# Forgetting attention: one 129-column product for upper probabilities in three of four query groups, the partial sums joined later, the division on GpSimd

## The chip, the cores and the metric

The kernel runs on one core of one Trainium2 chip. The metric is device time in microseconds (us) of one execution; the median of three runs before the change is 1155.76 us. Five engines work side by side, each through its own list of instructions in order: PE (TensorE, matrix products into PSUM), DVE (VectorE), ACT (ScalarE), POOL (GpSimd, which here also issues some transfers) and SP (SyncE, which issues most transfers). They wait for one another through semaphores.

## The reference

One decoder layer over 2048 tokens of width 1024. Eight heads of "forgetting" attention and eight heads of sliding-window attention share one input projection; both outputs are gated, projected, normalised and added to the input. The change lies in the forgetting attention:

```python
def one_block(args):
    qb, cb, n = args
    s = jnp.einsum('bhqd,bhkd->bhqk', qb, kh, preferred_element_type=jnp.float32) * scale
    s = s + cb[..., None] - cum[:, :, None, :]
    ...
    s = jnp.where(causal, s, -jnp.inf)
    p = jax.nn.softmax(s, axis=-1)
    return jnp.einsum('bhqk,bhkd->bhqd', p.astype(vh.dtype), vh)
```

All of it is to come out near f32 accuracy, so the kernel splits each f32 operand into an upper and a lower f16 part and adds three products (upper by upper, upper by lower, lower by upper).

## The kernel before

The program has three long stretches: projections with the sliding-window attention, up to about 450 us; the forgetting attention, from 450 to 987 us; the output projection after that. This text is about the second.

**Groups and steps.** A group is one head and one chunk of 512 queries (four query groups of 128, `u` 0 to 3). It is worked in steps of two key blocks of 128 each: 2, 4, 6 and 8 steps for the four chunks, 20 per head, 160 in all (`Step`). In a step, `scores` makes two pairs of products into the PSUM tile `sta` (L1330, L1331), `exp32` takes the exponential on ACT (L1335), on a diagonal step POOL masks it (L1339), `high` rounds it to the upper f16 part on ACT (L1343), `low` makes the lower part on DVE (L1346), and `pv` multiplies both parts with the values.

**The values.** `vt` holds, for each key block and head, 129 columns (`VW`): 64 of the upper part, a column of ones (64), and 64 of the lower part. The column of ones makes the sum of the probabilities in the same product. `pv` takes, for each key block and each `u`, three products into `poa`, a PSUM tile of four times 65 columns: upper probabilities by the upper values and the ones (65 columns, L1356), upper by lower values (64 columns, L1358, added onto the same columns), lower probabilities by upper values and ones (65 columns, L1359). There are 1088 pairs of a key block and a `u`; 768 of them belong to the first three `u`, 320 to the fourth. At the last step of a group DVE takes the reciprocal of the sums (L1363) and multiplies (L1365) into `ona`, and SP stores it (L1366). There is one `poa`: the next group's first product waits until DVE has read it.

**The order** is written out by hand in the loop over `steps`: in iteration s come `exp32` of s, a tick, `low` of s-1, the first half of the filling work, `high` of s, `scores` of s+1, a second tick, `pv` of s-2 (`PV_LAG`), the second half of the filling work. `after(n, f)` puts `f` off to the n-th tick from there. The filling work is products of later heads (L335, with their evacuations) and the search for row maxima of the next head's scores (products L1281, maxima on DVE L1284 and L1286), and it uses the PSUM tiles `bk`.

Of the kernel before, what the change touches and what calls it, by code (L numbers as in the profile page):

```python
# [10 lines left out]
F32 = mybir.dt.float32  # L11
# [3 lines left out]
AF = mybir.ActivationFunctionType  # L15
ALU = mybir.AluOpType
AX = mybir.AxisListType

P = 128
# [4 lines left out]
CH = 512  # L24
# [9 lines left out]
XM, XR, VW = 66, 69, 129  # L34
# [6 lines left out]
def hybrid_layer(  # L41
# [17 lines left out]
    V, A, G, PE, SP = nc.vector, nc.scalar, nc.gpsimd, nc.tensor, nc.sync  # L59
# [15 lines left out]
    o_d = [dram.tile([CH, D], F32, name=f"o_d{t}") for t in range(NCH)]  # L75
# [4 lines left out]
    def sm(n, tag):  # L80
        return small.tile([P, n], F32, tag=tag, name=tag)
# [106 lines left out]
    def after(n, f):  # L188
        late.append([n, f])
# [10 lines left out]
    first = ("kb", "vb", "zb0", "zb1")  # L200
# [253 lines left out]
    start = ExitStack()  # L454
# [241 lines left out]
    def swa_pool(name, bufs, **kw):  # L696
        return swa.enter_context(tc.tile_pool(name=name, bufs=bufs, reuse_waits="tile", **kw))

    op_ = swa_pool("op", 3)
# [149 lines left out]
    class Pair:  # L849
# [73 lines left out]
        def pv(self):  # L923
            j, i = self.j, self.i
            po = ps_pv.tile([P, 4, 64], F32, tag="pv", name="pob")
            for e, (i_, k0, nk) in enumerate(self.blocks):
                for h in range(2):
                    for b in range(nk):
                        for n, (pp_, vv) in enumerate(((0, 0), (0, 1), (1, 0))):
                            PE.matmul(po[:, 2 * e + h, :], self.ptt[:, pp_, self.at[e] + h * nk + b, :],  # L930
                                      vb[:, k0 + b, self.g, 64 * vv:64 * vv + 64],
                                      start=(b == 0 and n == 0), stop=(b == nk - 1 and n == 2))

            def out_():
                on = onp.tile([P, 2, P], F32, tag="on", name="on")
                V.tensor_tensor(on[:].rearrange("p e (h d) -> p (e h) d", h=2), po[:],
                                self.rinv[:].unsqueeze(2).broadcast_to([P, 4, 64]), op=ALU.mult)
                G.dma_start(o_d[i // 4][(i % 4) * P:(i % 4 + 2) * P, (4 + j) * P:(5 + j) * P]
                            .rearrange("(e p) c -> p e c", p=P), on[:])

            after(1, out_)
# [220 lines left out]
    def fox_pool(name, bufs, **kw):  # L1162
        return fox.enter_context(tc.tile_pool(name=name, bufs=bufs, reuse_waits="tile", **kw))

    ps_st = fox_pool("ps_st", 1, space=PSUM)
    ps_po = fox_pool("ps_po", 1, space=PSUM)
# [4 lines left out]
    op_ = foxl.enter_context(tc.tile_pool(name="opa", bufs=2, reuse_waits="tile"))  # L1171
# [77 lines left out]
    vt, lk, lq = fx["vt"], fx["lk"], fx["lq"]  # L1249
# [62 lines left out]
    class Step:  # L1312
# [35 lines left out]
        def pv(self):  # L1348
            hd, ph = self.hd, self.ph
            if self.first:  # L1350
                self.po_[0] = ps_po.tile([P, 4, 65], F32, tag="po", name="poa")
            po = self.po_[0]
            for n, (b, u0, o) in enumerate(self.blocks):
                for u in range(u0, 4):
                    pq = slice(o + (u - u0) * P, o + (u - u0 + 1) * P)
                    PE.matmul(po[:, u, :], ph[:, 0, pq], vt[:, b, hd, 0:65],  # L1356
                              start=(self.first and n == 0 and u == 0), stop=False)
                    PE.matmul(po[:, u, 0:64], ph[:, 0, pq], vt[:, b, hd, 65:VW], start=False, stop=False)  # L1358
                    PE.matmul(po[:, u, :], ph[:, 1, pq], vt[:, b, hd, 0:65], start=False,  # L1359
                              stop=(self.last and n == len(self.blocks) - 1))  # L1360
            if self.last:
                rinv = sm(4, "a_ri")
                V.reciprocal(rinv[:], po[:, :, 64])  # L1363
                on = op_.tile([P, 4, 64], F32, tag="ona", name="ona")
                V.tensor_tensor(on[:], po[:, :, 0:64], rinv[:].unsqueeze(2).broadcast_to([P, 4, 64]), op=ALU.mult)  # L1365
                SP.dma_start(o_d[self.ci][:, hd * 64:(hd + 1) * 64].rearrange("(u p) d -> p u d", p=P), on[:])  # L1366

        po_ = {}

# [213 lines left out]
    with tc.manual_schedule():  # L1583
# [29 lines left out]
        for s, stp_ in enumerate(steps):  # L1613
            hd, r = divmod(s, NS)
# [115 lines left out]
```

## Time and profile before

| | |
|---|---|
| median of three runs | 1155.76 us (1154.94 to 1155.79) |
| the profiled execution, its own time | 1155.56 us |
| its span in the trace | 1153.9 us |
| granted TensorE clock, mean | 0.995 |
| instructions | 27043 |
| ACT busy | 679.0 us (59%) |
| POOL busy | 166.4 us (14%) |

The time of the profiled execution is 1.66 us more than the span, which runs from the first to the last recorded instruction. "Busy" is the time in which an engine has an instruction in work; for PE the ends are modelled and products overlap, so that the start of one to the start of the next tells the pace, not the duration. In rows of a timeline the first column is the start in us from the span's start, the second the duration; a bracket names the idle time before it and what ended it.

### The profile page before, as it was taken

What the parts mean: (1) busy time and instruction counts of PE and PEld (TensorE: products, weight loads), DVE (VectorE), ACT (ScalarE), POOL (GpSimd) and SP (SyncE); (2) the same over time, 40 slices, a digit from 0 to 9 for tenths busy, and PEclk for the clock granted to TensorE, in tenths of its full rate; (3) what the DMA queues carried; (4) which work ended last, traced back from release to release, by engine and by line L of the source; (5) the groups of instructions that cost most, each with busy time, mean ns of one, the idle gap of its engine ahead of it and who ended that gap; (6) DMA issues with size and microseconds to landing.
All of it is one profiled execution on the core that took longest, in us unless ns stands there. A gap on an engine that the chain in (4) does not pass through costs nothing. (4 is left out here: it accounts for less than half of the span.)

```text
span 1153.9 us, 27043 instructions
## 1 busy us (share of the span) xinstructions
PE 1113.2 (96%) x10514; PEld 651.5 (56%) x10514; DVE 909.9 (79%) x2330; ACT 679.0 (59%) x1124; POOL 166.4 (14%) x302
## 2 busy tenths in 40 slices
PE   5899999999999999999999999999999989999997
PEld 1466657655579865555555555555555555455554
DVE  6776668879888477889888989878797886766666
ACT  4666446556666515766767667676776698233331
POOL 2011122234322101111111201101010010000000
PEclk9999999999999999999999999999999999999999
DMA  9646426587777423323233232313121264464642
GB/s 330 223 138 169 107 71 135 111 171 141 174 145 121 96 61 84 85 78 81 78 82 98 61 89 63 66 38 98 43 56 38 66 185 154 156 211 166 203 168 88
DMA packets 162452, 136.36 MB, mean 118 GB/s; under 512 B 95356, under 2 KB 139428, under 8 KB 162324
## 3 DMA queue, kind: packets, MB, share of 16 engines
q1 hardware_dynamic: 152388, 106.39, 35.3%
q0 software_dynamic: 9456, 27.72, 9.1%
q8 instruction: 82, 1.34, 0.5%
q10 hardware_dynamic: 480, 0.53, 0.2%
q14 instruction: 46, 0.38, 0.1%
HBM read 70.97 MB, written 25.18 MB: 83 GB/s over the span
## 5 line engine op out<-in xcount | busy, mean ns | idle before, releaser
L1335 ACT ACTIVATE p<-sta,lift,scl_qk 128x1024 f32<-128x1024 f32 (+2 forms) x160 | 172.0, 1075 | 94.6 <-PE sta L1331 88.7
L335 PE MATMUL bk<-hT,wh_qk 128*128 128x512 f16 x768 | 197.9, 378 | 0.6 <-DVE a_m L1284 0.6
L1503 PE MATMUL bk<-wohl,oz 128*128 128x512 f16 (+2 forms) x792 | 172.5, 372 | 2.2 <-DVE oz L1490 1.0
L1346 DVE TENSOR_TENSOR pha<-p,pha 128x1024 f16<-128x1024 f32 (+2 forms) x160 | 169.7, 1061 | 0.0
L1343 ACT ACTIVATE pha<-p 128x1024 f16<-128x1024 f32 (+2 forms) x160 | 148.1, 926 | 31.6 <-POOL p L1339 26.3
L1284 DVE TENSOR_REDUCE a_m<-bk 128x1 f32<-128x512 f32 x192 | 129.3, 683 | 36.3 <-PE bk L1281 35.4
L1503 PEld LDWEIGHTS <-oz 128*128 128x128 f16 x792 | 75.8, 99 | 83.2 <-issue 1.8
L1356 PE MATMUL poa<-vt,pha 128*128 128x65 f16 x1088 | 116.5, 193 | 1.6 <-DVE ona L1365 1.6
L1359 PE MATMUL poa<-vt,pha 128*128 128x65 f16 x1088 | 116.0, 192 | 1.3 <-DVE pha L1346 1.3
L1358 PE MATMUL poa<-vt,pha 128*128 128x64 f16 x1088 | 116.3, 194 | 0.0
L1330 PE MATMUL sta<-T 128*128 128x512 f16 (+1 forms) x320 | 109.6, 347 | 4.5 <-ACT p L1335 4.5
L1281 PE MATMUL bk<-T 66*128 66x512 f16 (+2 forms) x320 | 110.5, 348 | 2.2 <-DVE a_m L1284 2.2
L1356 PEld LDWEIGHTS <-pha 128*128 128x128 f16 x1088 | 101.6, 97 | 16.3 <-DVE ona L1365 2.9
L335 PEld LDWEIGHTS <-wh_qk 128*128 128x128 f16 x768 | 70.2, 97 | 71.6 <-issue 2.9
L1358 PEld LDWEIGHTS <-pha 128*128 128x128 f16 x1088 | 101.0, 97 | 13.4
L1331 PE MATMUL sta<-T 69*128 69x512 f16 (+1 forms) x320 | 108.0, 348 | 0.0
L1359 PEld LDWEIGHTS <-pha 128*128 128x128 f16 x1088 | 100.8, 99 | 1.6 <-DVE pha L1346 1.6
L335 PE MATMUL bk<-hT,wh_za 128*128 128x512 f16 x384 | 99.8, 378 | 0.0
L353 PE MATMUL bk<-wh_va,hT 128*128 128x128 f16 x1536 | 92.6, 219 | 0.0
L1339 POOL TENSOR_SCALAR_AFFINE_SELECT p<-p 128x256 f32<-128x256 f32 x64 | 31.9, 499 | 413.4 <-ACT p L1335 408.5
L335 PE MATMUL bk<-hT,wh_zb 128*128 128x512 f16 x384 | 90.8, 379 | 0.0
L353 PEld LDWEIGHTS <-hT 128*128 128x128 f16 x1536 | 87.5, 98 | 5.9 <-issue 3.5
(497 smaller groups left out, 1851.5 us busy)
## 6 DMA issues: line engine op xcount, KB each, us to landing
hT<-in_x_dram SPq DMA_DIRECT2D x20, 512.0 KB
wa<-in_w_ada_dram SPq DMA_DIRECT2D x16, 512.0 KB
T<-stq SPq DMA_DIRECT2D x128, 64.0 KB
T<-z_d SPq DMA_DIRECT2D x16, 512.0 KB
T<-o_d SPq DMA_DIRECT2D x16, 512.0 KB
z_d<-tz POOLq DMA_DIRECT2D x30, 256.0 KB, 2.9
out_dram<-hT SPq DMA_DIRECT2D x15, 512.0 KB
xt<-in_x_dram SPq DMA_DIRECT2D x12, 512.0 KB
```

Of the source, the lines that this page charges most:

```text
L335: PE.matmul(ps, whl[:, a, k, :], hT[ci][:, b, k, :], start=(k == 0 and n == 0), stop=(k == KT - 1 and n == 2))
L353: PE.matmul(ps[:, u * P:(u + 1) * P], hT[ci][:, a, k, u * P:(u + 1) * P], whl[:, b, k, :], start=(k == 0 and n == 0), stop=(k == KT - 1 an ...
L1281: PE.matmul(mx[:, :w], T[0:XM, 0, i * P:(i + 1) * P], T[0:XM, 2, pc * CH:pc * CH + w], start=True, stop=True)
L1284: V.tensor_reduce(m3[:, u, pc:pc + 1], mx[:, :w], axis=AX.X, op=ALU.max)
L1330: PE.matmul(self.st[:, o:o + w], T[:, 3, kb_], T[:, 1, qc], start=True, stop=False)
L1335: A.activation(self.p32[:, :self.w], self.st[:, :self.w], AF.Exp, scale=scl[f"qk{self.hd}"][:], bias=lift[:])
L1343: A.activation(self.ph[:, 0, :self.w], self.p32[:, :self.w], AF.Copy)
L1346: V.tensor_tensor(self.ph[:, 1, :self.w], self.p32[:, :self.w], self.ph[:, 0, :self.w], op=ALU.subtract)
L1356: PE.matmul(po[:, u, :], ph[:, 0, pq], vt[:, b, hd, 0:65], start=(self.first and n == 0 and u == 0), stop=False)
L1358: PE.matmul(po[:, u, 0:64], ph[:, 0, pq], vt[:, b, hd, 65:VW], start=False, stop=False)
L1359: PE.matmul(po[:, u, :], ph[:, 1, pq], vt[:, b, hd, 0:65], start=False, stop=(self.last and n == len(self.blocks) - 1))
L1503: PE.matmul(py, self.hl[:, i, k, :], w_slot(8 * j + k)[:, cc], start=(k == 0 and m_ == 0), stop=(k == KT - 1 and m_ == 2))
```

## The change

The tile `poa` becomes 512 columns wide. For `u` 0, 1 and 2 it holds 129 columns each: the upper probabilities are multiplied with all 129 columns of `vt` in one product, and the lower probabilities are added onto the first 65. For `u` = 3 the room is 65 columns (3 x 129 + 65 = 452), and the three products stay as they were. The sum over the upper and the lower values, which the products made before, is now taken after the group for the first three `u`: two copies on ACT (`by_u` columns 65 to 128, and the 64 columns of `u` 3) into `ona`, two reciprocals and one addition on DVE (`join`). The division is a product on POOL, followed by the store (`out_`). `join` stands at the first tick after the group's last `pv`, `out_` at the second.

```diff
@@ -1348,22 +1348,37 @@
         def pv(self):
             hd, ph = self.hd, self.ph
             if self.first:
-                self.po_[0] = ps_po.tile([P, 4, 65], F32, tag="po", name="poa")
+                self.po_[0] = ps_po.tile([P, CH], F32, tag="po", name="poa")
             po = self.po_[0]
             for n, (b, u0, o) in enumerate(self.blocks):
                 for u in range(u0, 4):
                     pq = slice(o + (u - u0) * P, o + (u - u0 + 1) * P)
-                    PE.matmul(po[:, u, :], ph[:, 0, pq], vt[:, b, hd, 0:65],
-                              start=(self.first and n == 0 and u == 0), stop=False)
-                    PE.matmul(po[:, u, 0:64], ph[:, 0, pq], vt[:, b, hd, 65:VW], start=False, stop=False)
-                    PE.matmul(po[:, u, :], ph[:, 1, pq], vt[:, b, hd, 0:65], start=False,
-                              stop=(self.last and n == len(self.blocks) - 1))
+                    c, first = u * VW, self.first and n == 0 and u == 0
+                    stop = self.last and n == len(self.blocks) - 1
+                    if u < 3:
+                        PE.matmul(po[:, c:c + VW], ph[:, 0, pq], vt[:, b, hd, 0:VW], start=first, stop=False)
+                    else:
+                        PE.matmul(po[:, c:c + 65], ph[:, 0, pq], vt[:, b, hd, 0:65], start=False, stop=False)
+                        PE.matmul(po[:, c:c + 64], ph[:, 0, pq], vt[:, b, hd, 65:VW], start=False, stop=False)
+                    PE.matmul(po[:, c:c + 65], ph[:, 1, pq], vt[:, b, hd, 0:65], start=False, stop=stop)
             if self.last:
+                on = op_.tile([P, 4, 64], F32, tag="ona", name="ona")
                 rinv = sm(4, "a_ri")
-                V.reciprocal(rinv[:], po[:, :, 64])
-                on = op_.tile([P, 4, 64], F32, tag="ona", name="ona")
-                V.tensor_tensor(on[:], po[:, :, 0:64], rinv[:].unsqueeze(2).broadcast_to([P, 4, 64]), op=ALU.mult)
-                SP.dma_start(o_d[self.ci][:, hd * 64:(hd + 1) * 64].rearrange("(u p) d -> p u d", p=P), on[:])
+                by_u = po[:, 0:3 * VW].rearrange("p (u c) -> p u c", u=3)
+
+                def join():
+                    A.activation(on[:, 0:3, :], by_u[:, :, 65:VW], AF.Copy)
+                    A.activation(on[:, 3, :], po[:, 3 * VW:3 * VW + 64], AF.Copy)
+                    V.reciprocal(rinv[:, 0:3], by_u[:, :, 64])
+                    V.reciprocal(rinv[:, 3:4], po[:, 3 * VW + 64:3 * VW + 65])
+                    V.tensor_tensor(on[:, 0:3, :], by_u[:, :, 0:64], on[:, 0:3, :], op=ALU.add)
+
+                def out_():
+                    G.tensor_tensor(on[:], on[:], rinv[:].unsqueeze(2).broadcast_to([P, 4, 64]), op=ALU.mult)
+                    SP.dma_start(o_d[self.ci][:, hd * 64:(hd + 1) * 64].rearrange("(u p) d -> p u d", p=P), on[:])
+
+                after(1, join)
+                after(2, out_)
 
         po_ = {}
```

In PE's list the first products of the first head's second group, with what they wait for (`pha` is the pair of probability parts, `poa` the PSUM tile, `sta` the scores; the names behind "waits" are engines' semaphores). Before:

```order
L1331 LDWEIGHTS T_6393
L1331 MATMUL sta<-T_6393 128x128
L1356 LDWEIGHTS pha [waits DVE_49]
L1356 MATMUL poa<-vt,pha 128x65 [waits PE_49]
L1358 LDWEIGHTS pha
L1358 MATMUL poa<-vt,pha 128x64
L1359 LDWEIGHTS pha
```

And now, at the same place:

```order
L1331 LDWEIGHTS T_6393
L1331 MATMUL sta<-T_6393 128x128
L1359 LDWEIGHTS pha [waits DVE_49,PE_49]
L1359 MATMUL poa<-vt,pha 128x129 [waits Activation_49]
L1363 LDWEIGHTS pha
L1363 MATMUL poa<-vt,pha 128x65
```

Three pairs of a weight load and a product became two for `u` 0 to 2; the wait for DVE is at a group's first weight load in both, and the first product now also waits for ACT, which reads `poa` too. (The new L1359 is the wide product, the new L1363 the one of the lower probabilities.)

In DVE's list the end of the first head's fourth group (the `pha` rows are `low` of two steps in sequence, the L1256 to L1261 rows are `key_limbs` of the next head). Before:

```order
L1346 TENSOR_TENSOR pha<-p_7913,pha 128x896
L1363 RECIPROCAL a_ri<-poa 128x4
L1365 TENSOR_TENSOR ona<-poa,a_ri 128x256
L1284 TENSOR_REDUCE a_m<-bk_139 128x1
L1256 TENSOR_SCALAR a_cv<-csum,isc_qk_7604 128x16
L1258 TENSOR_SCALAR lk<-a_cv 128x16
L1261 SCALAR_TENSOR_TENSOR a_cv<-lk,a_cv 128x16
L1258 TENSOR_SCALAR lk<-a_cv 128x16
L1261 SCALAR_TENSOR_TENSOR a_cv<-lk,a_cv 128x16
L1258 TENSOR_SCALAR lk<-a_cv 128x16
L1346 TENSOR_TENSOR pha<-p_7960,pha 128x384
```

And now:

```order
L1346 TENSOR_TENSOR pha<-p_7835,pha 128x896
L1284 TENSOR_REDUCE a_m<-bk_139 128x1
L1256 TENSOR_SCALAR a_cv<-csum,isc_qk_7560 128x16
L1258 TENSOR_SCALAR lk<-a_cv 128x16
L1261 SCALAR_TENSOR_TENSOR a_cv<-lk,a_cv 128x16
L1258 TENSOR_SCALAR lk<-a_cv 128x16
L1261 SCALAR_TENSOR_TENSOR a_cv<-lk,a_cv 128x16
L1258 TENSOR_SCALAR lk<-a_cv 128x16
L1372 RECIPROCAL a_ri<-poa 128x3
L1373 RECIPROCAL a_ri<-poa 128x1
L1374 TENSOR_TENSOR ona<-poa,ona 128x192
L1346 TENSOR_TENSOR pha<-p_7877,pha 128x384
```

DVE's last reading of `poa` moved behind the filling work of the second half of its iteration, to just ahead of the next `low`.

## The prediction

> **What bounds the kernel now.** The page first, then the windows and the waits of the stretch that the change touches, 450 to 987 us.
>
> ```profile
> span 1153.9 us, 27043 instructions
> ...
> PE 1113.2 (96%) x10514; PEld 651.5 (56%) x10514; DVE 909.9 (79%) x2330; ACT 679.0 (59%) x1124; POOL 166.4 (14%) x302
> ```
>
> ```profile
> 450.00:987.00 537.00, 525.59 (x5343) 298.01 (x5341) 459.68 (x997) 382.88 (x499) 66.04 (x117) 1.00 0.31 80
> ```
>
> ```profile
> PE sta L1330 <- ACT p L1335: 4.5, 6, 1.4
> PE poa L1356 <- DVE ona L1365: 1.6, 3, 0.9
> PE poa L1359 <- DVE pha L1346: 1.3, 2, 1.1
> PE bk L1281 <- DVE a_m L1284: 1.1, 1, 1.1
> ...
> PE bk L335 <- DVE a_m L1284: 0.6, 2, 0.4
> ```
>
> ```profile
> ACT p L1335 <- PE sta L1331: 88.7, 119, 2.1
> ```
>
> PE is busy 525.6 of these 537 us, DVE 459.7 (86%), ACT 382.9 (71%), all at clock 1.00; ACT waits 119 times for scores. So PE sets the time: what PE gains, the kernel gains, and each new wait on PE counts in full. DVE is the next engine, and PE already waits 4.6 us for it (1.6 + 1.3 + 1.1 + 0.6). An average of 86% doesn't say how late DVE is at one place; that is what the change asks.
>
> **What the products save.** Eight triples of a step, then two stretches of plain products, each with its own weight load:
>
> ```profile
> 702.62 0.19 PE L1356 MATMUL poa<-vt,pha 128*128 128x65 f16 x1
> ...
> 703.36 0.38 PE L335 MATMUL bk<-hT,wh_za 128*128 128x512 f16 x1
> ```
>
> ```profile
> 329.98 0.86 PE L930 MATMUL pob<-vb,ptb 128*128 128x64 f16 x24
> 330.68 2.84 PE L353 MATMUL bk<-wh_va,hT 128*128 128x128 f16 x48
> ```
>
> 24 products of 65, 64 and 65 columns take 703.36 - 702.62 = 0.74 us, 30.8 ns each and 92.5 ns a triple. The 128-column products of L353 last 219 ns each and 48 of them 2.84 us from the first start to the last end: (2.84 - 0.22) / 47 = 55.8 ns from start to start; 129 columns I put at 56.2. If the third product keeps its 30.8 ns, a triple of the first three query groups falls from 92.5 to 87.0, by 5.5 ns: 768 of them give 4.2 us. If instead the pair is charged at L930's pace (24 of 64 columns in 330.68 - 329.98 = 0.70 us, 29.2 ns each, 58.4 a pair), the gain is 2.2 ns: 1.7 us. No row shows 129 columns into a tile with odd strides; between the ends I take the middle, **-3.0 us**.
>
> A rule of the Trainium skill speaks against the change: the page "TensorE: Matmul & The Clock Gate", section "Back-to-back issue gap", gives about 81 ns for each 128-column product in a real stream of weight loads and products. By it the wide product would cost 81 - 61.6 = 19 ns more than the two it replaces, an estimate of +15 us over 768. L353's 55.8 ns, with a load for each product, doesn't bear it out here.
>
> **What the join costs by itself.**
>
> ```profile
> L1057 ACT ACTIVATE stq<-bk 128x512 f16<-128x512 f32 x32 | 18.9, 591 | 25.0 <-PE bk L335 24.7
> L784 ACT ACTIVATE vb<-bk 128x128 f16<-128x128 f32 x16 | 3.5, 274 | 8.7 <-PE bk L776 6.5 <-DVE xt L418 2.2
> ```
>
> ```profile
> L1363 DVE RECIPROCAL a_ri<-poa x32: 141/173/184, 454.8 to 987.4; 128x4 f32<-128x4 f32 x32
> L1365 DVE TENSOR_TENSOR ona<-poa,a_ri x32: 423/424/425, 455.0 to 987.7; 128x256 f32<-128x256 f32 x32
> ```
>
> ```profile
> L1476 DVE TENSOR_TENSOR T<-bk,T 128x512 f32<-128x512 f32 x32 | 20.6, 685 | 12.9 <-PE bk L1467 12.9
> ```
>
> ACT's copies from PSUM cost 274 ns at 128 columns and 591 at 512, 0.83 ns a column: 0.33 us for 192 and 0.22 for 64, 0.55 a group, 17.6 us over 32 groups. ACT has 88.7 us of waits for PE to hide them in. DVE loses 0.17 + 0.42 = 0.6 us a group and gets two reciprocals (0.35) and an addition of 192 columns (0.36, on the line through 424 ns at 256 and 685 at 512): 0.1 more. POOL is 66 of 537 us busy. Its division isn't in the trace; the nearest row:
>
> ```profile
> L1339 POOL TENSOR_SCALAR_AFFINE_SELECT p<-p x64: 396/406/1281, 436.5 to 981.2; 128x256 f32<-128x256 f32 x64
> ```
>
> I bound it by 0.4 and 2 us and take 1.3, the long end of that row, since it starts beside `low`. Only the store waits for it. SP's later rows stand behind that store; the tightest is a head's key tile:
>
> ```profile
> 873.78 0.60 SPq L1055 DMA_DIRECT2D T<-stq  x1
> ```
>
> ```profile
> 881.21 0.38 PE L1281 MATMUL bk<-T 66*128 66x512 f16 x1
> ```
>
> 7.4 us lie between its issue and its first use, more than the one iteration (537 / 160 = 3.4 us) and the division by which the store moves. All this costs nothing by itself; without that cover, late key tiles would hold PE some 1 us a head, 8 us.
>
> **What the join costs by its place.** This is the term that decides. PE may start a group only when DVE has read `poa`. Before, DVE did so right behind the last `pv` of the group before; now it first does the filling work of half an iteration. The end of the first head's fourth group, DVE then PE then ACT:
>
> ```profile
> 515.50 1.08 DVE L1346 TENSOR_TENSOR pha<-p,pha 128x896 f16<-128x896 f32 x1
> 516.50 0.18 DVE L1363 RECIPROCAL a_ri<-poa 128x4 f32<-128x4 f32 x1
> 516.71 0.42 DVE L1365 TENSOR_TENSOR ona<-poa,a_ri 128x256 f32<-128x256 f32 x1
> 517.05 0.68 DVE L1284 TENSOR_REDUCE a_m<-bk 128x1 f32<-128x512 f32 x1
> ...
> 518.83 0.55 DVE L1346 TENSOR_TENSOR pha<-p,pha 128x384 f16<-128x384 f32 x1
> ```
>
> ```profile
> 514.07 0.19 PE L1359 MATMUL poa<-vt,pha 128*128 128x65 f16 x1
> ...
> 517.19 0.20 PE L1356 MATMUL poa<-vt,pha 128*128 128x65 f16 x1
> ```
>
> ```profile
> 514.01 1.20 ACT L1335 ACTIVATE p<-sta,lift,scl_qk 128x1024 f32<-128x1024 f32 x1 [0.31 <-PE sta L1331]
> ```
>
> PE finishes the group's products at 514.26, but DVE reaches the reciprocal only at 516.50, 2.2 us late, and releases `poa` at 517.13; PE starts the next group at 517.19, just in time. ACT's exponential ends at 515.21, so its copies would be done by 515.8 and hold nobody. Now DVE does L1284 and the `key_limbs` rows first: 518.83 less the 0.6 taken out is 518.2, plus 0.7 for the join and 0.1 for the signal is 519.0. PE waits **1.8 us**. At another place there is room:
>
> ```profile
> 894.56 0.42 DVE L1365 TENSOR_TENSOR ona<-poa,a_ri 128x256 f32<-128x256 f32 x1
> ...
> 895.71 1.21 DVE L1346 TENSOR_TENSOR pha<-p,pha 128x1024 f16<-128x1024 f32 x1
> ```
>
> ```profile
> 896.59 0.19 PE L1356 MATMUL poa<-vt,pha 128*128 128x65 f16 x1
> ```
>
> 895.71 - 0.6 + 0.8 = 895.9, and PE comes at 896.59. I worked out the 31 places where another group follows in this way, with the copies' end as the bound where that is later: 20 are short, 11 have room. The first and the last short ones:
>
> ```profile
> 491.17 1.22 DVE L1346 TENSOR_TENSOR pha<-p,pha 128x1024 f16<-128x1024 f32 x1
> ```
>
> ```profile
> 490.52 0.19 PE L1356 MATMUL poa<-vt,pha 128*128 128x65 f16 x1
> ```
>
> ```profile
> 930.30 1.22 DVE L1346 TENSOR_TENSOR pha<-p,pha 128x1024 f16<-128x1024 f32 x1
> ```
>
> ```profile
> 930.44 0.20 PE L1356 MATMUL poa<-vt,pha 128*128 128x65 f16 x1 [0.92 <-DVE ona L1365]
> ```
>
> ```profile
> 509.52 0.70 DVE L1286 CUSTOM_DVE_ANT_0 bk<-bk,cmask 128x512 f32<-128x512 f32 x1 [0.89 <-PE bk L1281]
> ```
>
> They are short by 0.9 and 0.2; all 20 sum to 15.2 us. In six pairs DVE has no idle time between the two places (it last idled before 509.52 for the pair around 517), so a wait at the first lets it catch up for the second (after 517.19 the next place lacks 1.6, which the 1.8 covers). That leaves **+12.0 us**. Reading each place 0.4 us earlier or later gives 6.7 and 18.4.
>
> Two small terms: PE's gain made while DVE is late is waited away at the next short place, about half, **+1.5**; and a held PE meets fewer of the 3.0 us of other waits for DVE (1.3 + 1.1 + 0.6), a third, **-1.0**.
>
> **The sum**, against the profiled execution (1155.56, its span and 1.66 around it): 1155.56 - 3.0 + 12.0 + 1.5 - 1.0 = **1165.0**. The median shown is 0.2 above that execution; I leave 1165.0.
>
> **Rivals.** *DVE is not late* (ends at no change or faster). If DVE reaches the join 1.0 us earlier than I read, only the places with the largest lack remain, 2.3 us together, less than the 3.0 saved; at that point the sign turns. For it: DVE idles 14% and each wait of PE resets it. Against it: at 516.50 it is 2.2 us behind, without idle time for 7 us. With all waits gone, 1155.56 - 3.0 - 0.5 = 1152; with 3 us left, 1155.6. *The wide product is dear*: its weight load shows in full:
>
> ```profile
> L1356 PEld LDWEIGHTS <-pha 128*128 128x128 f16 x1088 | 101.6, 97 | 16.3 <-DVE ona L1365 2.9
> ```
>
> 97 - 61.6 = 35 ns on 768 is +27 us, near 1192 with the waits. Against it: 65-column products already go at 30.8 ns with the same loads. *Nothing is saved*: the wide product goes at the pace of its two parts; then only the waits show, 1166 to 1168, inside my range.
>
> **How the numbers follow.** Waits prevail 0.83 (with or without the saving), DVE catches up 0.15 (even 0.09, faster 0.06), dear product 0.02. The low end of the first case is 1155.56 - 4.2 + 6.7 + 0.5 = 1158.6, the high end 1155.56 - 1.7 + 18.4 + 0.5 = 1172.8; I widen to 1156 and 1174 to take in part of the even case and of longer waits. 0.2% (2.3 us) is about what a measurement of this kernel can tell from no change: faster 0.06, same 0.09, slower 0.85.
>
> **What would show it.** The wide products start 56 ns apart from the next one; PE's waits for DVE at the first product of a group rise from 1.6 us in 3 to about 12 in some 20, the largest ending at the fourth groups; DVE's join stands just before `low`; ACT's and POOL's new rows hold nobody. If those waits stay under 3 us, or if the wide products start 62 ns or more apart, a step above is wrong.

## The result, and the profile after

The changed kernel takes 1167.93 us (median of 4 runs, 1167.29 to 1170.08) beside 1155.62 us of the kernel before: a ratio of 1.0112, 95% interval 1.0098 to 1.0126. It is slower by about 1.1%. The prediction said 1165.0, between 1156 and 1174.

The head of the page of the kernel after, its two PE groups of the new upper and lower products, and the division on POOL:

```profile
span 1165.2 us, 25684 instructions
...
PE 1114.4 (96%) x9746; PEld 647.0 (56%) x9746; DVE 910.7 (78%) x2362; ACT 686.7 (59%) x1188; POOL 207.7 (18%) x334
...
L1363 PE MATMUL poa<-vt,pha 128*128 128x65 f16 x1088 | 113.4, 193 | 1.4 <-DVE pha L1346 1.4
...
L1359 PE MATMUL poa<-vt,pha 128*128 128x129 f16 x768 | 100.3, 220 | 11.1 <-DVE ona L1374 9.6
...
L1377 POOL TENSOR_TENSOR ona<-ona,a_ri 128x256 f32<-128x256 f32 x32 | 40.5, 1266 | 220.3 <-DVE ona L1374 72.7
```

PE's busy share tells nothing: 96% in both kernels. The span grew by 11.3 us, and the column behind the bar shows where: before the wide product PE now idles 11.1 us, where the first product of a group (then L1356) had 1.6.

Waits of PE in the forgetting attention (450 to 1000 us), in all, times, longest:

```profile
PE poa L1359 <- DVE ona L1374: 9.6, 12, 2.1
PE sta L1330 <- ACT p L1335: 5.7, 7, 1.4
PE bk L1518 <- DVE oz L1505: 1.8, 1, 1.8
PE poa L1363 <- DVE pha L1346: 1.4, 2, 1.2
PE poa L1359 <- ACT p L1335: 1.3, 1, 1.3
```

The 1.3 us put down to ACT in the last row are the join's too: at that place ACT's copies end at 727.02 us and DVE's addition at 729.35, and PE goes on at 729.49.

The place that the prediction worked out, the end of the first head's fourth group, in the timeline of the kernel after: DVE, PE and ACT.

```profile
515.87 0.68 DVE L1284 TENSOR_REDUCE a_m<-bk 128x1 f32<-128x512 f32 x1
...
517.65 0.17 DVE L1372 RECIPROCAL a_ri<-poa 128x3 f32<-128x3 f32 x1
517.74 0.14 DVE L1373 RECIPROCAL a_ri<-poa 128x1 f32<-128x1 f32 x1
517.79 0.34 DVE L1374 TENSOR_TENSOR ona<-poa,ona 128x192 f32<-128x192 f32 x1
518.05 0.55 DVE L1346 TENSOR_TENSOR pha<-p,pha 128x384 f16<-128x384 f32 x1
```

```profile
516.31 0.38 PE L1331 MATMUL sta<-T 69*128 69x512 f16 x1
518.28 0.22 PE L1359 MATMUL poa<-vt,pha 128*128 128x129 f16 x1 [1.59 <-DVE ona L1374]
518.34 0.19 PE L1363 MATMUL poa<-vt,pha 128*128 128x65 f16 x1
518.37 0.22 PE L1359 MATMUL poa<-vt,pha 128*128 128x129 f16 x1
518.42 0.19 PE L1363 MATMUL poa<-vt,pha 128*128 128x65 f16 x1
```

```profile
514.47 0.32 ACT L1370 ACTIVATE ona<-poa 128x192 f32<-128x192 f32 x1
514.68 0.22 ACT L1371 ACTIVATE ona<-poa 128x64 f32<-128x64 f32 x1
```

ACT has copied by 514.90. DVE first finds row maxima (L1284) and does the `key_limbs` rows left out here, and reads `poa` from 517.65 to 518.13. PE was ready at 516.5 and starts at 518.28.

**An account of PE.** Busy times of PE overlap, so I added up the time from each product's start to the next one's, from the first to the last product into `poa`. Where it is more than 25 ns over the pace of such a product, the excess is put down to the tile that the late product writes; the rest is work. (The pace is columns / 2.4 + 2.7 ns, which is 56 ns for 128 columns and 216 for 512, as the trace before has them. The few f32 products, 36 of 5347, were taken at four times that, though the trace has them at twice, 109 ns for 128 columns; this moves no entry by more than 0.1 us but e5's `bk`, by 0.6.) The view of waits above counts from a product's modelled end and lists fewer of the short waits, so its sums are smaller. In us, where the last column is the part of the two columns before it that lies in spells of half clock, as explained below:

| kernel | stretch | work on `poa` | waits at a group's first product | late into `bk` | late into `sta` | of these two, half clock |
|---|---|---|---|---|---|---|
| before | 536.7 | 100.3 | 2.4 | 11.0 | 6.8 | 0 |
| after | 549.2 | 96.8 | 14.4 | 13.5 | 8.1 | 1.7 |
| e1 | 551.0 | 100.4 | 15.6 | 11.9 | 6.8 | 1.7 |
| e2 | 537.2 | 96.8 | 1.0 | 13.4 | 9.6 | 0 |
| e4 | 550.4 | 96.9 | 15.1 | 14.2 | 7.2 | 2.5 |
| e5 | 614.1 | 97.4 | 59.8 | 27.0 | 7.5 | 20.2 |
| e6 | 542.1 | 96.8 | 0.2 | 19.7 | 9.1 | 0 |
| e7 | 544.0 | 100.5 | 1.9 | 17.8 | 7.3 | 1.0 |
| e8 | 534.5 | 96.8 | 0.2 | 13.4 | 7.7 | 0 |
| e10 | 536.4 | 100.2 | 0.2 | 12.4 | 7.2 | 0 |

The change itself, second row less first: 3.5 us less work, 12.0 more waits at first products, 3.8 more in the two columns for `bk` and `sta`; the stretch is 12.5 us longer. (It starts 0.8 us earlier and what follows it is 0.3 us shorter, so the span grew by 11.3.)

**Half clock.** These two columns are not all waits. The granted TensorE clock is 1.00 in nearly all of the stretch, but 0.50 in spells of 3.4 us: one in after, one in e1, two in e4, one in e7, 17 in e5, none in before, e2, e6, e8 and e10. Three products of 512 columns of one line in after, ahead of its spell and in it, and then a window over the spell (its third number from the end is the granted clock):

```profile
585.68 0.81 PE L335 MATMUL bk<-hT,wh_qk 128*128 128x512 f16 x3
...
590.52 1.48 PE L335 MATMUL bk<-hT,wh_qk 128*128 128x512 f16 x3
```

```profile
590.10:593.50 3.40, 3.40 (x13) 1.17 (x11) 1.72 (x3) 1.46 (x2) 1.33 (x3) 0.50 0.60 154
```

In after and in e1 the spell begins 0.6 and 0.7 us behind the first product that waited longest, 2.3 us; in e5 each of the 17 begins during such a wait, of 2.0 to 3.9 us, or within 1.3 us of its end, while two more waits of that size bring none. The second spell of e4 and the one of e7 follow shorter waits. That the wait brings the half clock about is read from this order and was not tried by itself. Without the half clock the waits into `bk` and `sta`, the "other waits" below, are 17.8 us before, 19.9 in after and 17.0 in e1.

### The profile page after: what moved, and what is told of

It is laid out like the page before. It is cut to its first block, busy times and chain, and to the rows that moved or that the text cites. A ratio compares the mean times of both kernels' runs of the same rounds, so it can differ in the third digit from the quotient of the medians.

```text
span 1165.2 us, 25684 instructions
## 1 busy us (share of the span) xinstructions
PE 1114.4 (96%) x9746; PEld 647.0 (56%) x9746; DVE 910.7 (78%) x2362; ACT 686.7 (59%) x1188; POOL 207.7 (18%) x334
## 3 DMA queue, kind: packets, MB, share of 16 engines
q8 instruction: 76, 1.25, 0.5%
## 5 line engine op out<-in xcount | busy, mean ns | idle before, releaser
L1518 PE MATMUL bk<-wohl,oz 128*128 128x512 f16 (+2 forms) x792 | 172.5, 372 | 3.0 <-DVE oz L1505 1.8
L1284 DVE TENSOR_REDUCE a_m<-bk 128x1 f32<-128x512 f32 x192 | 129.8, 684 | 43.3 <-PE bk L1281 42.6
L1518 PEld LDWEIGHTS <-oz 128*128 128x128 f16 x792 | 75.8, 99 | 83.9 <-DVE oz L1505 2.2
L1363 PE MATMUL poa<-vt,pha 128*128 128x65 f16 x1088 | 113.4, 193 | 1.4 <-DVE pha L1346 1.4
L1359 PE MATMUL poa<-vt,pha 128*128 128x129 f16 x768 | 100.3, 220 | 11.1 <-DVE ona L1374 9.6
L1363 PEld LDWEIGHTS <-pha 128*128 128x128 f16 x1088 | 96.6, 98 | 13.5 <-DVE pha L1346 1.9
L335 PE MATMUL bk<-hT,wh_qb 128*128 128x512 f16 x384 | 88.9, 379 | 0.0
L1359 PEld LDWEIGHTS <-pha 128*128 128x128 f16 x768 | 70.9, 97 | 30.7 <-issue 9.5
L1286 DVE CUSTOM_DVE_ANT_0 bk<-bk,cmask 128x128 f32<-128x128 f32 (+3 forms) x128 | 63.2, 494 | 30.3 <-PE bk L1281 29.3
L1377 POOL TENSOR_TENSOR ona<-ona,a_ri 128x256 f32<-128x256 f32 x32 | 40.5, 1266 | 220.3 <-DVE ona L1374 72.7
```

What stands on the lines that cost most here:

```text
L335: PE.matmul(ps, whl[:, a, k, :], hT[ci][:, b, k, :], start=(k == 0 and n == 0), stop=(k == KT - 1 and n == 2))
L1284: V.tensor_reduce(m3[:, u, pc:pc + 1], mx[:, :w], axis=AX.X, op=ALU.max)
L1359: PE.matmul(po[:, c:c + VW], ph[:, 0, pq], vt[:, b, hd, 0:VW], start=first, stop=False)
L1363: PE.matmul(po[:, c:c + 65], ph[:, 1, pq], vt[:, b, hd, 0:65], start=False, stop=stop)
L1518: PE.matmul(py, self.hl[:, i, k, :], w_slot(8 * j + k)[:, cc], start=(k == 0 and m_ == 0), stop=(k == KT - 1 and m_ == 2))
```

## The experiments

The theory: PE loses its time because DVE lets go of `poa` half an iteration later, and DVE is late there. The rivals: POOL's division beside DVE's work, ACT's copies, or the wide product itself. All times are medians, beside the kernel before run on the same chip (1155.49 us for e1, e2, e4 and e5, 1155.55 for the others).

**e1: the late release alone**, on the kernel before.

```diff
+                def join():
-                V.reciprocal(rinv[:], po[:, :, 64])
+                    V.reciprocal(rinv[:], po[:, :, 64])
...
+                after(1, join)
+                after(2, out_)
```

> The kernel before with one edit: its reciprocal and product on DVE move to the first tick after the group's last products, the store to the second; products, ACT and POOL stay as before. Late release (my theory): PE's waits at a group's first product rise from 1.6 us in 3 to about 10 in a dozen, and the time to 1167 (1164 to 1170), since nothing is saved on the products. If the POOL division, the ACT copies or the wide product made the loss: 1155 to 1157.

Measured: 1169.07 us (1.0116, 1.0102 to 1.0130). PE's waits at the first products, and DVE's rows, in the trace of e1:

```profile
PE poa L1356 <- DVE ona L1367: 11.7, 13, 2.2
```

```profile
L1366 DVE RECIPROCAL a_ri<-poa x32: 168/174/184, 455.6 to 1002.5; 128x4 f32<-128x4 f32 x32
L1367 DVE TENSOR_TENSOR ona<-poa,a_ri x32: 423/424/425, 455.8 to 1002.7; 128x256 f32<-128x256 f32 x32
```

The same two DVE instructions with the same durations as before, only later in the list, cost 13.6 us (with the spell at half clock that its trace has, 1.7 us). No wide product, no copy and no division on POOL is in this kernel.

**e2: the same order, but released by ACT.** One copy moves all 452 columns to SBUF; everything else reads the copy. The tile is twice as large, so there is one buffer instead of two.

```diff
-                on = op_.tile([P, 4, 64], F32, tag="ona", name="ona")
+                sv = op_.tile([P, 4, VW], F32, tag="ona", name="ona", bufs=1)
...
+                    A.activation(sv[:].rearrange("p u c -> p (u c)")[:, 0:3 * VW + 65], po[:, 0:3 * VW + 65], AF.Copy)
+                    V.reciprocal(rinv[:], sv[:, :, 64])
+                    V.tensor_tensor(sv[:, 0:3, 0:64], sv[:, 0:3, 0:64], sv[:, 0:3, 65:VW], op=ALU.add)
```

> The kernel after, but one ACT copy of the 452 columns into SBUF (one buffer, taking twice the room) is all that reads poa; reciprocal and addition stay on DVE at the same place, the division on POOL. Late release: ACT lets go of poa some 1.5 us ahead of the next group's first product, PE's waits there fall under 3 us, the products' saving of 3 to 4 us shows: 1152.5 (1151 to 1155). If POOL's division or DVE's added work made the loss, both are still there: 1164 to 1168.

Measured: 1156.03 us (1.0006, 0.9997 to 1.0015), above the range expected. Nearly all of the loss is gone with DVE's rows at their late place and POOL's division still there, which decides between theory and rivals. But the 3.5 us saved on the products don't show. Two rows of its waits, of PE and of ACT, and ACT's copy:

```profile
PE bk L1479 <- DMA T<-o_d: 1.2, 1, 1.2
```

```profile
ACT ona L1369 <- DMA o_d<-ona: 3.3, 2, 1.6
```

```profile
L1369 ACT ACTIVATE ona<-poa x32: 534/537/548, 454.7 to 987.6; 128x452 f32<-128x452 f32 x32
```

ACT waited twice for the store of the group before to leave the one buffer, and in the last head the output stage waited for rows that were stored late, behind POOL's division. e8 takes both waits away.

**e4: the division on DVE** instead of POOL, right behind the addition.

```diff
+                    V.tensor_tensor(on[:], on[:], rinv[:].unsqueeze(2).broadcast_to([P, 4, 64]), op=ALU.mult)
...
-                    G.tensor_tensor(on[:], on[:], rinv[:].unsqueeze(2).broadcast_to([P, 4, 64]), op=ALU.mult)
```

> The kernel after with the division on DVE right behind the addition instead of on POOL. Late release: poa is released at the same place, so 1167 (1165.5 to 1169), waits at the first products within 2 us of after. If POOL's division costs by contention with DVE's next operation or by delaying the masks and the stores: it falls by the 4 us by which the other waits of PE grew, to 1163 or lower.

Measured: 1167.91 us (1.0105, 1.0091 to 1.0119), the time of after.

```profile
PE poa L1359 <- DVE ona L1374: 10.0, 12, 2.1
PE sta L1330 <- ACT p L1335: 4.9, 6, 1.4
```

POOL's division costs nothing that the medians show. The other waits are 18.9 us here and 19.9 in after, both without the half clock; 0.7 of the difference is one wait for output rows stored late (the row of after follows). It is in after, e2 and e6, which divide on POOL, and in no kernel that divides on DVE:

```profile
PE bk L1482 <- DMA T<-o_d: 0.7, 1, 0.7
```

**e5: later still.** `after(2, join)` instead of `after(1, join)`.

> The kernel after with the join at the second tick instead of the first, behind one more lower part (1.2 us) and the filling work of half an iteration on DVE, still ahead of the next group's first product in the program. Late release: each of the 31 places comes 1 to 2.5 us later, part of it shared by neighbours: 1195 (1180 to 1215). If the place doesn't matter: within 1.5 us of after.

Measured: 1232.71 us (two runs; 1.0668, 1.0649 to 1.0688), above the range expected.

```profile
PE poa L1359 <- DVE ona L1374: 48.5, 26, 3.8
```

Another half iteration costs 65 us, five times the first. The table has 45 us of it at first products. Another 24, which I had not counted, are products at half clock: 20.2 in the last column and 5.0 on products into `poa`, less the 1.7 of after; the mean granted clock is 0.973, against 0.995. The other waits didn't grow but fell, from 19.9 to 14.3 us.

**e8: e2 with the division on DVE**, so that the store can go at once.

```diff
+                    V.tensor_tensor(sv[:, :, 0:64], sv[:, :, 0:64], rinv[:].unsqueeze(2).broadcast_to([P, 4, 64]), op=ALU.mult)
...
-                    G.tensor_tensor(sv[:, :, 0:64], sv[:, :, 0:64], rinv[:].unsqueeze(2).broadcast_to([P, 4, 64]), op=ALU.mult)
```

> e2 with the division on DVE behind the addition, in the same SBUF tile, so that the store can go at the second tick without POOL. If what e2 still lacked (3.5 us saved on the products, but no gain in time) went into the one buffer that ACT waits for (3.3 us in two waits) and into the late store of the last head: 1153 (1152 to 1154.5). If it is ACT's added 17 us that delay the exponentials: 1156 as before.

Measured: 1153.11 us (0.9983, 0.9974 to 0.9991): faster than both kernels, by 2.4 us than before. At the place shown above (ACT, DVE and PE of e8):

```profile
514.58 0.54 ACT L1369 ACTIVATE ona<-poa 128x452 f32<-128x452 f32 x1
```

```profile
517.75 0.17 DVE L1370 RECIPROCAL a_ri<-ona 128x4 f32<-128x4 f32 x1
517.84 0.33 DVE L1371 TENSOR_TENSOR ona<-ona 128x192 f32<-128x192 f32 x1
518.21 0.43 DVE L1372 TENSOR_TENSOR ona<-ona,a_ri 128x256 f32<-128x256 f32 x1
```

```profile
516.41 0.38 PE L1331 MATMUL sta<-T 69*128 69x512 f16 x1
516.63 0.22 PE L1359 MATMUL poa<-vt,pha 128*128 128x129 f16 x1
```

DVE is as late as in the kernel after (517.75), but PE goes on at 516.63, because ACT was done with `poa` at 515.12.

**e10: e8 with the products of before**, a copy of 260 columns and no addition.

> e8 with the three products of before (65, 64 and 65 columns for every query group) and so a copy of 260 columns and no addition. It differs from e8 in the wide product and what that makes necessary. If the wide product saves what the trace says (100.3 to 96.8 us between starts): 3.5 us above e8, 1156 to 1157. If the saving is eaten by the longer copy and the addition: within 1 us of e8.

Measured: 1155.83 us (1.0001, 0.9992 to 1.0010), 2.7 us above e8. The products save 3.4 us (100.2 against 96.8); 1.5 us of that comes back as other waits (12.4 + 7.2 against 13.4 + 7.7).

**e6 and e7: two tiles `poa`**, paid for with one of the five `bk`; e7 is the kernel before with four `bk`.

```diff
-    ps_po = fox_pool("ps_po", 1, space=PSUM)
+    ps_po = fox_pool("ps_po", 2, space=PSUM)
...
-    bk += [ps_bx.tile([P, CH], F32, name=f"bk{n}") for n in (3, 4)]
+    bk += [ps_bx.tile([P, CH], F32, name=f"bk{n}") for n in (3,)]
```

> The kernel after with two tiles poa in turn, for which one of the five tiles bk goes. Late release: PE's waits at first products vanish (under 1 us); beside e7, which has the same tiles bk, it is faster by the products' 3.5 us and the 1.6 us that before waits: 3 to 6 us under e7. If the loss came from ACT's, DVE's or POOL's added work: above e7 by 7 us or more.

> Control for e6: the kernel before with four tiles bk instead of five. It prices the missing tile alone; both theories expect a slower kernel, by a few us to 30 us through waits of PE for a free bk, and its number is the base for e6.

Measured: e6 1165.57 us (1.0089, 1.0073 to 1.0104), e7 1164.52 us (1.0077, 1.0064 to 1.0091). With a second tile the waits at first products are gone (0.2 us in the table), and e6 is not the 7 us above e7 that the rivals asked for. But it isn't 3 to 6 us below it either; the intervals overlap. Rows of e6's waits of PE:

```profile
PE sta L1330 <- ACT p L1335: 6.2, 7, 1.4
PE bk L1518 <- DVE oz L1505: 1.8, 1, 1.8
PE bk L1482 <- DMA T<-o_d: 1.7, 1, 1.7
```

In e7 the scores wait 4.5 us, L1503 (the line that is L1518 in e6) 1.0, and the third row isn't there: 4.2 us more in e6 by these rows, 4.7 by the table without the half clock, somewhat more than the 3.7 that its products save. The profiled runs differ by 2.2 us of span in e6's favour. Of these, 1.3 are the spell at half clock that the profiled e7 has and the profiled e6 hasn't (1.0 in the column, 0.3 on products into `poa`); what is left, 0.9, and the medians, 1.1 in e7's favour, still don't agree to 2 us. So the pair shows the waits gone, and not what the change is worth without them.

## Why the prediction was right

- **What bounds the kernel.** Right: a wait added to PE counted in full (e1: 13.2 us more waits at first products, 13.6 us more time). What the prediction doesn't have is that the granted clock can fall to half behind a long wait: 1.7 us in after and in e1.
- **The products.** -3.0 forecast, -3.5 measured from start to start. The wide product is followed by the next start after 57 ns (median of 768) and the 65-column one after 29, against the 56.2 and 30.8 of the prediction. The Trainium skill's 81 ns for 128 columns ("TensorE: Matmul & The Clock Gate", section "Back-to-back issue gap") isn't what this stream does either: the trace speaks against the rule.
- **The join by its place.** 12.0 us more waits at first products were measured. Forecast were +12.0 from the places and +1.5 for gain that is waited away there, 13.5 together, since the second term lies in the same waits. Place by place: 1.8 forecast after the first head's fourth group, 1.75 measured; the first short place lacked 0.9 and cost 0.4; the last lacked 0.2 on top of the 1.1 that it waited before, and cost 1.25. Some 20 short places were forecast; 21 of the 31 first products start late. The credit for neighbouring places held in the main: the second of the pair around 517 lost 0.5 instead of 1.6, where the credit had left nothing. So a list of DVE's rows between two places, with what leaves it and what joins it, and PE's time of arrival, was enough to size the loss. That 12.0 stands on both sides is luck: single places are off by up to 0.5 us either way.
- **The join by itself.** ACT's copies at 0.32 and 0.22 us, the reciprocals at 0.17 and 0.14 and the addition at 0.34 were priced within 0.04. But "All this costs nothing by itself" was not so. Where ACT lets go of `poa` in time and no spell of half clock falls, the other waits still rise from 17.8 us to 19.6 with a copy of 260 columns on ACT and the old products (e10), and to 21.1 with 452 columns and the wide products (e8); after has 19.9.
- **The two small terms.** "A held PE meets fewer of the other waits, -1.0": with the late release alone they did fall, by 0.8 (e1, without the half clock), but in the changed kernel they rose by 2.1, with ACT's copies, the faster products and the late store. The "+1.5" is not seen as a term of its own. So the median lies 2.9 us above the forecast because of two things that the sum lacks, half clock (+1.7) and other waits (+2.1 in place of -1.0), less the 1.5 and the 0.5 by which waits at first products and products came out better. These are differences of single profiled runs, and what raised the other waits isn't taken further apart.
- **The rivals.** "DVE is not late" fell at first sight of the waits. "The wide product is dear" fell with the 57 ns. The division on POOL took 1.3 us in the mean, as assumed, and held PE for 0.7 us in all, through a late store.

## What to carry to other kernels

When an evacuation is moved, ask which tile it lets go of and what its engine has queued ahead of it at the new place: an engine that is 86% busy on average can be 2 us late exactly there, and a test that moves only the release (e1) shows it at once. If there is only one such tile, let the engine that arrives first copy it out in one instruction and do the arithmetic on the copy; here that, with the division back on DVE, turned a loss of 12 us into a gain of 2.4 us (e8). A few us saved on the bounding engine aren't worth a new wait of it for the next busy one. And when gaps between starts are added up as waits, look at the granted clock in those windows first: products at half clock look the same.

## What the runs showed that I had not expected

The price of lateness is far from straight: half an iteration later costs 13.6 us (e1), a second half 65 us more (e5). The first half iteration was partly covered by room: in after 21 of the 31 first products start late, by 0.7 us in the mean. In e5 all 31 do, by 1.9 us, and 17 times the granted clock is 0.50 for 3.4 us at such a wait, which makes products 25 us longer in all.

Durations of POOL's division and of DVE's lower parts in the kernel after (least, median, most):

```profile
L1377 POOL TENSOR_TENSOR ona<-ona,a_ri x32: 612/1453/1467, 455.3 to 1000.4; 128x256 f32<-128x256 f32 x32
L1346 DVE TENSOR_TENSOR pha<-p,pha x160: 544/1212/1295, 443.8 to 998.1; 128x1024 f16<-128x1024 f32 x96, 128x896 f16<-128x896 f32 x32, 128x384 f16<-128x384 f32 x32
```

The division takes 0.61 us the one time that no `low` runs beside it, and 1.45 in the median. Beside `low` it lasts some 0.47 us longer than the two overlap: 0.79 at an overlap of 0.32, 1.46 at 0.99. `low` keeps its 1.21 us: of the two it is POOL that yields. The Trainium skill ("GPSIMD Engine Reference", section "1. Specifications") says that GpSimd shares its SBUF interfaces with VectorE and that VectorE instructions with two SBUF inputs contend for them; the trace agrees, and shows which side pays.
